# Keeping the low parts of layer 1's weights in DRAM, and casting them on ScalarE

## The chip, the cores and the metric

The kernel runs on one core of one Trainium2 chip. The metric is the device time of one execution in microseconds; three runs of the kernel before have a median of 985.02 us (984.18 to 985.11). Engines are named as in the profile: PE is the matrix engine (TensorE, PEld its weight loads), DVE is VectorE, ACT is ScalarE, POOL is GpSimd, SP is SyncE, which issues nearly all transfers.

## The reference

A decoder trunk of two layers over 1024 positions and 1024 channels, in float32. Layer 0 mixes by causal pooling, layer 1 by attention in a window of 128 with one sink per head.

```python
# layer 0
h = rmsnorm(x) * (1 + scale) + shift            # shift, scale, gate = silu(c) @ ada_w + ada_b
u, z = split(h @ w_in)                          # 2 x 2048 channels
y = group_matmul(causal_multiscale_pool(u)) * a_scale
x = x + gate * ((y * silu(z)) @ w_out)          # the output product of layer 0
# one K and V for layer 1, from x
kv = (rmsnorm(x) * kv_g * (1 + kscale) + kshift) @ w_kv
# layer 1
q, z = split(h @ b_w_in)                        # 16 heads of 64
o = windowed_attention(q, k, v, rel_bias, sinks)
x = x + gate * ((o * silu(z)) @ b_w_out)
return rmsnorm(x) * final_g
```

## The kernel before

**High and low parts.** PE multiplies in a shortened form of float32. So that the product keeps its precision, every operand is split in two: a high part (the value cast to that form) and a low part (the value less its high part). A product is three matmuls: high by high, high by low, low by high. Activations are split once. A weight tile is 128 x 1024 (512 KB); it is loaded as `raw`, ScalarE casts it to `wh`, and VectorE subtracts to `wl`. The tags `raw`, `wh` and `wl` have two buffers each.

**The stages.** Until about 424 us come the input products and the pooling of layer 0. From 424 to 565 us runs layer 0's output product: 16 steps, `order` = (n, hf), n the block of 128 output channels and hf the half of the inputs; steps with n < 5 compute both halves q of the positions (48 matmuls), the last six only the first half (24 matmuls). The second half of n = 7, 6, 5 follows until about 599 us (`last_chunk`), beside the first normalisation for layer 1. Each step needs one weight tile from `wao`. Beside the steps, `ada_step` loads a row block of the modulation weights (`ada_rest`) into a `tmp` tile, and VectorE takes its dot product with c (L239). The list ADA says how many after each step. `tmp` has three buffers, used in turn.

**Layer 1** is a list `specs` of steps that PE runs in this order. For each half q of the positions and each group r of four heads: `queries` (two weight tiles of `wb`), `gates` (two), and `start`, which sets the attention of the four blocks of 128 positions going; `attend` is a generator whose parts (scores; transposes of the probabilities; product with V) are put between the matmuls of later steps at times of a counted clock. `keys` and `values` use `wkv`. `project_out(q, part)` multiplies the attention's output by the four weight tiles `wbo[part]`; `residual` (L686) adds it to x, and for part 1 ScalarE squares the new x and GpSimd adds up the squares in `sqh` (L195). `stats` has PE sum `sqh` over the channels (L142) for the last normalisation; `finish` applies it and stores. The weights of `wbo[1]` are loaded twice: once in steps, once by `load_last` into kept tiles `wo` that the last steps (`out_quarter`) use.

**Who sets the order.** In the output product and in layer 1 the order of PE is as written; that of the other engines comes from a scheduler that knows costs and priorities. Every engine and SyncE's queue then run their own instructions strictly in that order.

Of the kernel before, what the change touches and what calls it, by code (L numbers as in the profile page):

```python
# [12 lines left out]
F32 = mybir.dt.float32  # L13
# [5 lines left out]
P = 128  # L19
D = 1024  # L20
T = 1024
# [24 lines left out]
ADA = (0, 0, 0, 2, 4, 4, 4, 4, 4, 4, 1, 1, 1, 1, 0, 0)  # L46

ENDS = (0, 1, 3, 5, 7)

# [6 lines left out]
def trunk(ctx, tc, xT, c, pack, ada_first, ada_rest, wu0_in, wg0_in, wa, wg, wao, wkv,  # L56
# [8 lines left out]
    sp = ctx.enter_context(tc.tile_pool(name="small", bufs=2))  # L65
    pp = ctx.enter_context(tc.tile_pool(name="psum", bufs=1, space=PSUM))

    BANKS = {"d": 4, "S": 2, "tp": 1, "o": 1}
# [64 lines left out]
    def load_w(src):  # L133
        return split_w(*fetch(src))

    def rstd_stats(sq, n, more=None):
# [81 lines left out]
    with ExitStack() as sa:  # L218
# [580 lines left out]
        with tc.manual_schedule(engines={ET.PE}):  # L799
# [29 lines left out]
            def half_w(n, hf):  # L829
                return load_w(wao[n, hf])  # L830

            def g_acts(hf):
# [3 lines left out]
                     + [(n, hf) for n in range(2, KT) for hf in range(2)])  # L836
            ws, outs = {}, {}
            ws[0, 0] = half_w(0, 0)
            gather(4, 5, 6, 7)
            for i, (n, hf) in enumerate(order):  # L840
# [14 lines left out]
                for _ in range(ADA[i]):  # L855
                    ada_step()
                if hf == 1:
                    for q in qs:
                        residual(n, q, outs[n][q], 16)
                    for q in qs:  # L860
                        square_add(n, q)
            assert rest_at[0] == len(rest_cols)
            mod_scale(8, 56, C_KVG)
# [150 lines left out]
    def keys(q, hk, ps=None):  # L1014
# [9 lines left out]
        if ps is not None:  # L1024
            return done(ps)
        return wkv[0], lambda w: gemm_steps(w, 0, hk, KT, done)

    vts = {}

    def values(q, hk, ps=None):  # L1030
        def done(ps):
            vts[q] = bp.tile([P, H], F32, tag="ol", name="vt", bufs=1)
            nc.scalar.copy(out=vts[q], in_=ps)
        if ps is not None:
            return done(ps)
        return wkv[1], lambda w: gemm_steps(w, 0, hk, KT, done)

# [14 lines left out]
    def queries(q, r, j, h1):  # L1052
        def run(w):
# [12 lines left out]
            yield from gemm_steps(w, 0, h1, KT, done)  # L1066
        return wb[2 * r + j], run

    def gates(q, r, j, h1):
        def run(w):  # L1070
# [10 lines left out]
            yield from gemm_steps(w, 0, h1, KT, done)  # L1081
        return wb[8 + 2 * r + j], run

# [82 lines left out]
    def out_part(q, part, n2):  # L1166

        def run(w):
            acts = lambda k, i: qts[q, 2 * part + k // 2][:, k % 2, i, :]
            for i in range(2):  # L1170
# [6 lines left out]
                yield from gemm_steps(w, i * 512, acts, 4, done)  # L1177
        return wbo[part, n2], run

# [148 lines left out]

    def woven(l, at):

        r = []
        for i, x in enumerate(l):
            r.append(x)
            if i in at:
                r.append(bare(load_last))
        return r

    keys(0, hk0, got["pswk"])
# [24 lines left out]
    with tc.manual_schedule(engines={mybir.EngineType.PE}):  # L1363
        srcs = [i for i, sp_ in enumerate(specs) if sp_[0] is not None]
        loaded = {srcs[0]: got["wq"]}
        for i, (src, run) in enumerate(specs):
# [65 lines left out]
```

## Time and profile before

| | |
|---|---|
| median of 3 runs | 985.02 us |
| profiled execution | 984.87 us |
| its span, first to last instruction | 982.6 us |
| PE, VectorE, ScalarE, GpSimd busy | 961.9, 775.7, 458.1, 145.0 us |
| granted clock of PE | 0.996 |
| read from HBM, written to it | 111.2 MB, 13.6 MB |

Busy times are those of the engine with anything running, so PE's 98% says that it is seldom idle, not that it is at its peak. A row of a window gives, for a stretch of the span, busy time and instructions of each engine, the clock, the share of time that the 16 DMA engines were busy, and what they moved. A row of waits gives who waited for whom: us in total, times, longest.

### The profile page before, as it was taken

To read this page: it belongs to the slowest core of one execution; us is meant where nothing else is said; L and a number is where in the kernel's file an instruction comes from. 1 tells how busy PE (TensorE), PEld (TensorE's weight loads), DVE (VectorE), ACT (ScalarE), POOL (GpSimd) and SP (SyncE) were. 2 spreads that over 40 slices of the span, in tenths; PEclk is the share of its full clock that TensorE was granted. 3 is DMA by queue.
4 is the path that set the end of the run, shared out by engine and by line. 5 is a ranking of instruction groups with operands and counts; after the bars stand their busy time and mean duration, and the time that the engine had idled before them with its cause. 6 is when DMAs were issued, how large, how long until landed. Compare 5 with 4: busy or idle time off the path is not lost.

```text
span 982.6 us, 12696 instructions
## 1 busy us (share of the span) xinstructions
PE 961.9 (98%) x4538; PEld 801.2 (82%) x4538; DVE 775.7 (79%) x1411; ACT 458.1 (47%) x902; POOL 145.0 (15%) x173
## 2 busy tenths in 40 slices
PE   8999999999999999999999999999999999999996
PEld 6788888888888887888888888877888888887786
DVE  5897978677978699676782278599899878889985
ACT  6534434333433244551111145486677546566544
POOL 2100000000000000000000000052324313335723
PEclk9999999999999999999999999999999999999998
DMA  9453622264225411779861223222211221223222
GB/s 331 183 174 114 192 103 65 78 201 150 65 85 194 150 64 57 262 267 327 305 216 65 86 64 130 86 65 69 82 66 64 87 86 65 64 88 106 86 87 86
DMA packets 40625, 125.67 MB, mean 128 GB/s; under 512 B 4465, under 2 KB 6641, under 8 KB 40434
## 3 DMA queue, kind: packets, MB, share of 16 engines
q1 hardware_dynamic: 40416, 123.82, 37.6%
q10 hardware_dynamic: 146, 1.05, 0.3%
q8 instruction: 35, 0.57, 0.2%
q14 instruction: 28, 0.23, 0.1%
HBM read 111.22 MB, written 13.63 MB: 127 GB/s over the span
## 4 chain that ended last, share of the span: by engine, by line
PE 78%; DVE 16%; issue 2%; ACT 2%; POOL 1%; DMA 0%; POOLq 0%; DVEq 0%; SPq 0%; ACTq 0%
PE ps_d L214 14%; PE ps_S L214 9%; PE ps_d L636 9%; PE ps_d L203 6%; PE ps_d L204 6%; PE ps_d L205 6%; PE ps_S L636 4%; PE ps_o L214 4%; PE ps_tp L214 3%; DVE wl L123 2%; PE ps_d L374 2%; PE ps_o L636 2%; PE ps_tp L636 2%; DVE tmp L542 2%; PE ps_tp L1125 1%
## 5 line engine op out<-in xcount | busy, mean ns | idle before, releaser
L121 ACT CAST wh<-raw 128x1024 fp32r<-128x1024 f32 x73 | 76.5, 1048 | 101.4 <-PE ps_d L214 78.5
L123 DVE TENSOR_TENSOR wl<-raw,wh 128x1024 fp32r<-128x1024 f32 x73 | 94.2, 1290 | 26.7 <-ACT wh L121 22.8
L203 PE MATMUL ps_d<-hm,wh 128*128 128x512 f32 x288 | 113.8, 395 | 0.0
L205 PE MATMUL ps_d<-hm,wl 128*128 128x512 f32 x288 | 112.4, 390 | 0.3 <-DVE wl L123 0.3
L204 PE MATMUL ps_d<-hm,wh 128*128 128x512 f32 x288 | 112.4, 390 | 0.0
L239 DVE CUSTOM_DVE_ANT_0 tmp<-tmp,cact,pk 128x1024 f32<-128x1024 f32 x48 | 60.7, 1282 | 33.2 <-DMA tmp<-ada_rest 32.9
L214 PE MATMUL ps_d<-gh,wh 128*128 128x512 f32 x224 | 82.0, 389 | 0.0
L214 PE MATMUL ps_S<-gh,wh 128*128 128x512 f32 x192 | 64.5, 390 | 0.0
L205 PEld LDWEIGHTS ps_d<-hm,wl 128*128 128x128 f32 x288 | 54.1, 188 | 12.6 <-DVE wl L123 1.1
L636 PE MATMUL ps_d<-hs,ws 128*128 128x512 f32 x264 | 63.4, 389 | 0.0
L1115 ACT ACTIVATE pt<-pt,nm 128x129 f32<-128x129 f32 x128 | 50.2, 394 | 26.8 <-DVE nm L1111 24.6
L203 PEld LDWEIGHTS ps_d<-hm,wh 128*128 128x128 f32 x288 | 54.1, 188 | 10.2
L204 PEld LDWEIGHTS ps_d<-hm,wh 128*128 128x128 f32 x288 | 54.2, 188 | 10.0
L636 PEld LDWEIGHTS ps_d<-hs,ws 128*128 128x128 f32 x264 | 49.5, 188 | 10.3
L542 DVE TENSOR_TENSOR tmp<-tmp 128x1039 f32<-128x1039 f32 (+3 forms) x40 | 49.4, 1235 | 6.8 <-ACT tmp L672 5.7
L612 ACT CAST ws<-tw 128x512 fp32r<-128x512 f32 x44 | 26.8, 621 | 53.9 <-PE ps_tp L214 15.1
L636 PE MATMUL ps_d<-ha,ws 128*128 128x512 f32 x216 | 51.9, 389 | 0.0
L534 POOL MEMSET tmp<- 128x16 f32 x16 | 1.7, 111 | 331.4 <-DVE tmp L542 115.9
L214 PEld LDWEIGHTS ps_d<-gh,wh 128*128 128x128 f32 x224 | 42.1, 188 | 8.7
L636 PEld LDWEIGHTS ps_d<-ha,ws 128*128 128x128 f32 x216 | 40.5, 188 | 8.4
L147 POOL TENSOR_TENSOR rs<-v,mhalf 128x4 f32<-128x4 f32 (+1 forms) x7 | 8.2, 1164 | 241.6 <-DVE v L145 241.6
L214 PE MATMUL ps_d<-gh,wl 128*128 128x512 f32 x112 | 43.6, 389 | 0.0
(294 smaller groups left out, 2492.0 us busy)
## 6 DMA issues: line engine op xcount, KB each, us to landing
tmp<-ada_rest SPq DMA_DIRECT2D x48, 512.0 KB, 4.7
raw<-wb SPq DMA_DIRECT2D x32, 512.0 KB, 3.3
raw<-wa SPq DMA_DIRECT2D x28, 512.0 KB, 3.7
raw<-wao SPq DMA_DIRECT2D x20, 512.0 KB, 4.1
ad<-ada_first SPq DMA_DIRECT2D x16, 512.0 KB, 5.0
x<-xT SPq DMA_DIRECT2D x32, 256.0 KB, 5.9
raw<-wbo SPq DMA_DIRECT2D x16, 512.0 KB, 3.3
kept_g<-tmp SPq DMA_DIRECT2D x14, 512.0 KB, 2.9
```

What stands on the lines that cost most here:

```text
L121: nc.scalar.copy(out=wh, in_=raw)
L123: nc.vector.tensor_sub(out=wl, in0=raw, in1=wh.bitcast(F32))
L203: mm(ps, lh, acts(k, 0), start=k == 0, stop=False)
L204: mm(ps, lh, acts(k, 1), start=False, stop=False)
L205: mm(ps, ll, acts(k, 0), start=False, stop=k == n - 1)
L214: mm(p, lhs, acts(k, hl, q), start=start and k == 0 and s == 0, stop=stop and k == n - 1 and s == 2)
L239: nc.vector.tensor_tensor_reduce(out=raw, in0=raw, in1=ca, scale=0.5, scalar=pk[:, bcol:bcol + 1], op0=ALU.mult, op1=ALU.add, accum_out=ad ...
L374: mm(psu[i, q], w0[k // 2][:, k % 2, w, i * P:(i + 1) * P], block(k, q)[hl], start=k == 0 and s == 0, stop=k == KT - 1 and s == 2)
L542: nc.vector.tensor_add(out=nx[:, 2 * s - 1:], in0=cur[:, 2 * s - 1:], in1=cur[:, s - 1:PAD + T - s])
L612: nc.scalar.copy(out=ws[i][:, 0, :], in_=src)
L636: mm(ps, lhs, acts(k, hl), start=start and k == 0 and s == 0, stop=k == 3 and s == 2, skip_group_check=True)
L1115: nc.scalar.activation(pt[:, i, :P + 1], pt[:, i, :P + 1], AF.Exp, bias=nm[:, i:i + 1], scale=-1.0, accum_out=den[:, i:i + 1])
```

## The change

Three things, in layer 0's output product and in layer 1:

- Behind the steps of the output product, `stage` makes the low part of 18 weight tiles of layer 1 (all 16 of `wb`, both of `wkv`): load into a `tmp` tile, cast on ScalarE into a `stage` tile, subtract on VectorE, store to a tile in DRAM (`kept_l`). The list STAGED says how many after each step.
- In layer 1 a weight whose low part is kept is loaded as two tiles, raw and low part, and ScalarE casts both. Weights are fetched two steps ahead instead of one, with a second pair of raw buffers (`raw1`). The four tiles `wbo[0]` are split as before at their first use, and their low parts stored then; at the second use they are loaded.
- `wbo[1]` is loaded and split once, into the kept tiles `wo`, in the steps of `project_out(0, 1)`; `load_last` is gone. The first step of `project_out(1, 0)` now stands ahead of `project_out(0, 1)`.

```diff
+STAGED = (0, 0, 0, 0, 0, 1, 2, 3, 3, 3, 1, 1, 1, 1, 1, 1)
...
+    kp = ctx.enter_context(tc.tile_pool(name="kept", bufs=1, space=bass.MemoryType.DRAM))
...
+    kept_l = {}
+
+    def keep(key, lo):
+        kept_l[key] = kp.tile([P, 1024], F32, name="kl")
+        nc.sync.dma_start(kept_l[key], lo.bitcast(F32))
...
+            staged = [("b", i) for i in (1, 8, 9, 2, 3, 10, 11)] + [("kv", 0), ("kv", 1)] + [
+                ("b", i) for i in (4, 5, 12, 13, 6, 7, 14, 15, 0)]
+            stage_hi = []
+
+            def stage():
+
+                name, i = key = staged.pop(0)
+                raw = tmp()[:, :1024]
+                nc.sync.dma_start(raw, {"b": wb, "kv": wkv}[name][i])
+                hi = stage_hi[len(staged) % 2].rearrange("p a c -> p (a c)")
+                nc.scalar.copy(out=hi, in_=raw)
+                lo = raw.bitcast(F32R)
+                nc.vector.tensor_sub(out=lo, in0=raw, in1=hi.bitcast(F32))
+                keep(key, lo)
...
                 for _ in range(ADA[i]):
                     ada_step()
+                if STAGED[i] and not stage_hi:
+                    stage_hi += [slot("stage") for _ in range(2)]
+                for _ in range(STAGED[i]):
+                    stage()
...
-    def load_last():
-
-        raw = wp.tile([P, 1024], F32, tag="raw", name="raw")
-        nc.sync.dma_start(raw, wbo[1, len(last_w)])
-        w = hp.tile([P, 2, T], F32R, tag="h", name="wo")
-        nc.scalar.copy(out=w[:, 0, :], in_=raw)
-        nc.gpsimd.tensor_sub(out=w[:, 1, :], in0=raw, in1=w[:, 0, :].bitcast(F32))
-        last_w.append((w[:, 0, :], w[:, 1, :]))
+    def fetch_any(key):
+
+        src = (wb if key[0] == "b" else wkv if key[0] == "kv" else wbo)[key[1:]]
+        pool, tag = ((wp, "raw"), (bp, "raw1"))[fetched[0] % 2]
+        fetched[0] += 1
+        r = [pool.tile([P, 1024], F32, tag=tag, name=tag, bufs=2) for _ in range(2)]
+        nc.sync.dma_start(r[0], src)
+        if key in kept_l:
+            nc.sync.dma_start(r[1], kept_l[key])
+        return key, r
+
+    def split_any(key, r):
+
+        if key[0] == "o" and key[1]:
+            t = hp.tile([P, 2, T], F32R, tag="h", name="wo")
+            w = t[:, 0, :], t[:, 1, :]
+            last_w.append(w)
+        else:
+            w = [wp.tile([P, 1024], F32R, tag=t, name=t) for t in ("wh", "wl")]
+        nc.scalar.copy(out=w[0], in_=r[0])
+        if key in kept_l:
+            nc.scalar.copy(out=w[1], in_=r[1])
+        else:
+            nc.vector.tensor_sub(out=w[1], in0=r[0], in1=w[0].bitcast(F32))
+            if key[0] == "o" and not key[1]:
+                keep(key, w[1])
+        return w
...
-        *woven(project_out(0, 1) + project_out(1, 0)[:2], (0, 2, 4, 6)),
+        *project_out(1, 0)[:2],
+        *project_out(0, 1),
         stats(0), project_out(1, 0)[2], finish(0, 4, FINISH[0]),
...
-                    loaded[srcs[nxt]] = load_w(specs[srcs[nxt]][0])
+                    loaded[srcs[nxt]] = split_any(*raw)
+                if nxt + 1 < len(srcs):
+                    raw = fetch_any(specs[srcs[nxt + 1]][0])
```

Lines of the kernel move down by 10 at L142 and by 29 or more in layer 1, so L142 is L152 after the change, L121 and L123 are L124 and L126, and L253 is L263.

SyncE's queue, the last transfers of the output product before the change: modulation rows, then nothing but weights (`wao` those of this product, `wkv` and `wb` of layer 1).

```order
L253 DMA tmp<-ada_rest 128x1024 x6
L130 DMA raw<-wao 128x1024
L253 DMA tmp<-ada_rest 128x1024 x5
L130 DMA raw<-wao 128x1024
L253 DMA tmp<-ada_rest 128x1024 x5
L130 DMA raw<-wao 128x1024 x10
L130 DMA raw<-wkv 128x1024 x2
```

The same place after the change, from the last but two modulation rows on. `tmp<-wb` is the load of a staged tile, `kl<-tmp` the store of its low part; the first `wao` row here is the load for the last of the 16 steps.

```order
L263 DMA tmp<-ada_rest 128x1024
L133 DMA raw<-wao 128x1024
L144 DMA kl<-tmp 128x1024
L856 DMA tmp<-wb 128x1024
L263 DMA tmp<-ada_rest 128x1024
L856 DMA tmp<-wb 128x1024
L133 DMA raw<-wao 128x1024
L144 DMA kl<-tmp 128x1024
L856 DMA tmp<-wb 128x1024
L144 DMA kl<-tmp 128x1024
L856 DMA tmp<-wb 128x1024
L133 DMA raw<-wao 128x1024
L144 DMA kl<-tmp 128x1024 x2
```

Loads and stores of the staging now stand between the weights of the output product; a load into `tmp` stands there until the buffer of the third tile before it is free.

PE's rows around the statistics of the first half, before the change: the products ahead of it belong to (1, 0) (weights in `wh`, `wl`).

```order
L203 MATMUL ps_d<-qt,wh 128x512
L204 MATMUL ps_d<-qt,wh 128x512
L205 MATMUL ps_d<-qt,wl 128x512
L142 MATMUL ps_o<-invd,sqh 128x1 x4
L203 MATMUL ps_d<-qt,wh 128x512
```

After the change the products directly ahead of it are those of (0, 1) (weights in the kept `wo`), whose squares it sums.

```order
L213 MATMUL ps_d<-qt,wo 128x512
L214 MATMUL ps_d<-qt,wo 128x512
L215 MATMUL ps_d<-qt,wo 128x512
L152 MATMUL ps_o<-invd,sqh 128x1 x4
L213 MATMUL ps_d<-qt,wh 128x512
```

The 24 matmuls of one step of (1, 0) that stood between are gone from there. On VectorE, the residual of that last product (L696) after the change stands behind an attention step, and the statistics (L155) behind it:

```order
L1184 SCALAR_TENSOR_TENSOR of<-ps_o,ol 64x256 x2
L1158 TENSOR_TENSOR cur<-ps_tp,cur 128x512
L1188 TENSOR_TENSOR of<-of,szb 128x256
L1136 COPY_PREDICATED ps_S<-tri,ps_S 128x2x128 x2
L1190 TENSOR_TENSOR qt<-of,qt 128x2x128
L1140 ISA pt,nm<-ps_S,bias,nsink 128x128
...
L696 SCALAR_TENSOR_TENSOR x<-ps_d,adac,x 128x512
L1147 RECIPROCAL den<-den 128x4
L1148 TENSOR_TENSOR pt<-pt,den 128x4x128
L155 TENSOR_SCALAR v<-ps_o 128x4
```

Where the line of dots is stand three more instructions L1140 and the reads of their results. Before the change the statistics (L145) came right behind a residual of (1, 0).

More of the change, by code (lines that the diff above doesn't have):

```diff
@@ L861, in trunk @@
                         square_add(n, q)
-            assert rest_at[0] == len(rest_cols)
+            assert rest_at[0] == len(rest_cols) and not staged
             mod_scale(8, 56, C_KVG)
@@ L1025, in keys @@
             return done(ps)
-        return wkv[0], lambda w: gemm_steps(w, 0, hk, KT, done)
+        return ("kv", 0), lambda w: gemm_steps(w, 0, hk, KT, done)
     vts = {}
@@ L1035, in values @@
             return done(ps)
-        return wkv[1], lambda w: gemm_steps(w, 0, hk, KT, done)
+        return ("kv", 1), lambda w: gemm_steps(w, 0, hk, KT, done)
     def values_split(q):
@@ L1066, in run @@
             yield from gemm_steps(w, 0, h1, KT, done)
-        return wb[2 * r + j], run
+        return ("b", 2 * r + j), run
     def gates(q, r, j, h1):
@@ L1081, in run @@
             yield from gemm_steps(w, 0, h1, KT, done)
-        return wb[8 + 2 * r + j], run
+        return ("b", 8 + 2 * r + j), run
     done_blocks = set()
@@ L1177, in run @@
                 yield from gemm_steps(w, i * 512, acts, 4, done)
-        return wbo[part, n2], run
+        return ("o", part, n2), run
     def bare(f):
@@ L1216, in trunk @@
     last_w = []
-    def load_last():
-        raw = wp.tile([P, 1024], F32, tag="raw", name="raw")
-        nc.sync.dma_start(raw, wbo[1, len(last_w)])
-        w = hp.tile([P, 2, T], F32R, tag="h", name="wo")
-        nc.scalar.copy(out=w[:, 0, :], in_=raw)
-        nc.gpsimd.tensor_sub(out=w[:, 1, :], in0=raw, in1=w[:, 0, :].bitcast(F32))
-        last_w.append((w[:, 0, :], w[:, 1, :]))
+    fetched = [0]
+    def fetch_any(key):
[22 more added lines that the diff above has]
+        return w
     def stats_quarter(c):
@@ L1327, in project_out @@
         return [ready(q, part)] + [out_part(q, part, n2) for n2 in range(4)]
[L1329 to L1336, printed above, removed]
     keys(0, hk0, got["pswk"])
@@ L1365, in trunk @@
         loaded = {srcs[0]: got["wq"]}
+        raw = fetch_any(specs[srcs[1]][0])
         for i, (src, run) in enumerate(specs):
```

## The prediction, written before the change was run

> **What bounds the kernel now.** I read the page first (busy time, then the 40 slices), after it the waits of the matrix engine, and then the stages one by one.
>
> ```profile
> span 982.6 us, 12696 instructions
> PE 961.9 (98%) x4538; PEld 801.2 (82%) x4538; DVE 775.7 (79%) x1411; ACT 458.1 (47%) x902; POOL 145.0 (15%) x173
> DVE 5897978677978699676782278599899878889985
> ACT 6534434333433244551111145486677546566544
> DMA 9453622264225411779861223222211221223222
> ```
>
> PE is busy in 98% of the span, so almost all time that this change can give back is the little that PE waits for others. The slices (24.6 us each) show two different places: in slices 17 to 21 (about 393 to 516 us: the start of layer 0's output product) the DMA engines are full while VectorE and ScalarE have room; in layer 1 (from about 600 us) it is the other way round. The change moves VectorE work from the second place to the first, and pays for it in transfers. PE's waits in layer 1 are all there is to win:
>
> ```profile
> engine line waited for: us in total, times, longest us
> PE ps_tp L1125 <- DVE pt L1119: 6.1, 5, 1.6
> PE ps_tp L154 <- DVE cur L1129: 0.4, 1, 0.4
> PE ps_d L205 <- DVE wl L123: 0.3, 1, 0.3
> PE ps_S L1105 <- DVE qt L1063: 0.3, 1, 0.3
> ```
>
> That is the whole list from 599 to 972 us: 7.1 us, every row naming VectorE. The same list over the output product (424 to 565 us) is empty: there PE waits for nobody. How full the DMA engines are there, in stretches of that stage (columns: stretch, then busy us of PE, PEld, DVE, ACT, POOL, granted clock, DMA share, GB/s):
>
> ```profile
> 439.00:467.00 28.00, 28.00 (x126) 23.17 (x125) 15.06 (x23) 3.38 (x4) 0.00 (x0) 1.00 0.92 321
> 467.00:489.00 22.00, 22.00 (x99) 18.22 (x98) 18.15 (x27) 3.66 (x5) 0.00 (x0) 1.00 0.87 300
> 489.00:511.00 22.00, 22.00 (x99) 18.22 (x98) 16.54 (x27) 3.62 (x5) 0.00 (x0) 1.00 0.83 271
> 511.00:533.00 22.00, 22.00 (x99) 18.22 (x98) 6.71 (x9) 3.61 (x5) 0.00 (x0) 1.00 0.16 54
> 533.00:565.00 32.00, 32.00 (x143) 26.50 (x142) 10.81 (x13) 6.92 (x9) 0.00 (x0) 1.00 0.26 83
> ```
>
> Until 511 us the engines are 83 to 92% taken by what is there already (30 loads for the dot products of the later modulation, the weights, x); after that the queue is nearly empty for 54 us. So the added transfers have about 54 us of free queue to go into.
>
> **Part 1: the low parts made beside the output product.** Each of 18 steps adds a load of 512 KB, a cast on ScalarE, a subtraction on VectorE and a store of 512 KB. The rows that price them:
>
> ```profile
> L121 ACT CAST wh<-raw 128x1024 fp32r<-128x1024 f32 x73 | 76.5, 1048 | 101.4 <-PE ps_d L214 78.5
> L123 DVE TENSOR_TENSOR wl<-raw,wh x15: 1212/1221/1226, 425.3 to 555.3; 128x1024 fp32r<-128x1024 f32 x15
> L239 DVE CUSTOM_DVE_ANT_0 tmp<-tmp,cact,pk x30: 1276/1284/1287, 445.9 to 511.3; 128x1024 f32<-128x1024 f32 x30
> DMA packets 6521, 21.56 MB, mean 299 GB/s; under 512 B 717, under 2 KB 717, under 8 KB 6518
> q1 hardware_dynamic: 6518, 21.52, 87.4%
> tmp<-ada_rest SPq DMA_DIRECT2D x30, 512.0 KB, 4.9
> raw<-wao SPq DMA_DIRECT2D x7, 512.0 KB, 5.0
> kept_g<-tmp SPq DMA_DIRECT2D x14, 512.0 KB, 2.9
> 554.22 1.06 ACT L121 CAST wh<-raw 128x1024 fp32r<-128x1024 f32 x1 [4.34 <-PE ps_d L214]
> ```
>
> On the engines it is cheap: 18 x 1.05 = 18.9 us of ScalarE and 18 x 1.22 = 22.0 us of VectorE, where ScalarE idles most of the time. I cost that at nothing; its cover is PE's 140 us of matmuls, and between 511 and 565 us VectorE is busy only 17.5 of 54 us. The transfers are the cost. Bytes before, from 439 to 565 us: 28 x 321 + 22 x 300 + 22 x 271 + 22 x 54 + 32 x 83 = 25.4 MB. Added: 36 x 0.524 = 18.9 MB. Together 44.3 MB, all through one queue that SyncE issues in order. The weights that PE needs stand in the same queue: behind the load for the last of the 16 steps (n = 7, second half) only 12 transfers (6.3 MB) of this stage follow, so 38.0 MB must go ahead of it. Step 15's cast of wh starts at 554.22, when step 13 frees the buffer, and step 14 has 24 matmuls of 32.00/143 = 0.224 us, 5.4 us; so PE wants its weights at about 559.9. From issue to ready it takes 5.0 to land, 1.05 to cast, 1.22 to subtract: 7.3 us. The load must therefore be issued by 552.6, and 38.0 MB from 439 on in 113.6 us is 334 GB/s. Against that stand 321 GB/s (best stretch), 299 (mean of 439 to 511 us) and 299/0.874 = 342 with no gap at all. PE is late by 38.0/rate - 113.6: 4.8 us at 321, 13.5 at 299, nothing at 342. I take 310, between the two measured stretches, since the new stores keep three tmp buffers busy longer (below): 122.6 us, **9.0 us late**, range 0 to 13.5.
>
> The buffers say the same from another side. A dot product holds one of three tmp buffers for 4.9 + 1.28 = 6.2 us; a staged tile holds it for 4.9 + 1.05 + 1.22 + its store (2.9 in a quiet queue, 4.9 as an estimate from the loads in this full one) = 10.1 to 12.1 us. 30 of the one and 18 of the other are 368 to 404 us of holding, over three buffers 123 to 135 us: 439 to 562 or 574 if none ever waits. And SyncE stands still at a load whose buffer isn't free, with the weights behind it. A rule of the Trainium skill (HBM Reference, Specifications) says that a core streaming alone measures about 425 GB/s, well above its 358 share; at 425 the 38.0 MB take 89 us and this term is zero. The trace doesn't bear it out: no stretch of this stage passes 321 at 0.92 busy.
>
> **Part 2: layer 1 with 37 subtractions fewer.** VectorE does 45 weight subtractions in the steps of layer 1 now (first row below, from 599 us on); 31 + 2 (queries, gates, keys, values) and 4 (second use of the first output weights) become ScalarE casts, so VectorE loses 37 x 1.22 = 45 us and ScalarE gains 37 casts less the 4 of the weights that are loaded once: 33 x 1.05 = 35 us. GpSimd loses its 4 subtractions. PE can gain at most the 7.1 us. Where its waits lie:
>
> ```profile
> L123 DVE TENSOR_TENSOR wl<-raw,wh x45: 1186/1226/2104, 612.3 to 937.7; 128x1024 fp32r<-128x1024 f32 x45
> L123 DVE TENSOR_TENSOR wl<-raw,wh x3: 1210/1671/2089, 647.1 to 663.8; 128x1024 fp32r<-128x1024 f32 x3
> 640.00:670.00 30.00, 26.75 (x135) 22.20 (x134) 29.08 (x58) 26.16 (x50) 18.81 (x15) 1.00 0.22 71
> PE ps_tp L1125 <- DVE pt L1119: 3.3, 2, 1.6
> PE ps_tp L1125 <- DVE pt L1119: 0.5, 1, 0.5
> 888.00:926.00 38.00, 35.72 (x184) 29.91 (x184) 34.69 (x71) 22.05 (x50) 27.14 (x21) 1.00 0.31 97
> PE ps_tp L1125 <- DVE pt L1119: 2.3, 2, 1.5
> ```
>
> (The three wait rows are of 640 to 670, 670 to 690 and 890 to 926 us.) From 640 to 670 VectorE is busy 29.08 of 30 us, but ScalarE 26.16 too: three splits lie there (second row), and three more casts make it 29.3. The wait moves rather than goes; I take half of 3.3. The 0.5, the 2.3 (GpSimd's subtractions go as well) and the 0.3 for wl I let go: **4.8 us gained**, range 7.1 gained to 3.3 lost (ScalarE's queue delays the exponentials as VectorE's did). The second load of each pair lies on a queue that the slices show 1 to 3 tenths busy, and is fetched a step earlier than now: nothing. The four stores of low parts in the first output step each hold a wl buffer for some 3 us more, beside matmuls of 5.4 us: nothing.
>
> **Part 3: the statistics right behind their last product.** The new order puts the four output steps (0,1) behind the first step of (1,0), so the statistics matmul of the first half comes straight after the product that it needs. Before, 24 matmuls stood between, and it was just in time:
>
> ```profile
> 920.06 3.32 POOL L195 TENSOR_TENSOR sqh<-sqh,sq 128x512 f32<-128x512 f32 x2 [2.62 <-ACT sq L191]
> 924.04 0.95 PE L142 MATMUL ps_o<-invd,sqh 128*128 128x1 f32 x8
> 902.08 0.40 PE L203 MATMUL ps_d<-qt,wh 128*128 128x512 f32 x1
> 906.80 0.74 DVE L686 SCALAR_TENSOR_TENSOR x<-ps_d,adac,x 128x512 f32<-128x512 f32 x1
> 907.62 0.19 ACT L1115 ACTIVATION_READ_ACCUMULATOR pt<-pt,nm 128x1 f32 x1
> 908.65 0.63 ACT L191 ACTIVATE sq<-x 128x512 f32<-128x512 f32 x1
> L195 POOL TENSOR_TENSOR sqh<-sqh,sq x7: 1284/1299/2274, 898.3 to 922.1; 128x512 f32<-128x512 f32 x7
> ```
>
> GpSimd's last sum ended at 923.38, PE asked at 924.04. In the new order PE asks 9 matmuls after an attention step's scores. A round of the same kind starts at 902.08: nine matmuls later it is 904.1. But the residual of that product stands on VectorE behind the attention step's eleven instructions and ran at 906.80 to 907.54; ScalarE was through with the exponentials at 907.81, and the square waited for a cast of wo that is gone there: 907.8 to 908.4. GpSimd's sum adds 1.28: 909.7. Wait 909.7 - 904.1 = **5.5 us**; at most 6.5 with the trace's own square (909.28 + 1.28), at least 0.74 + 0.63 + 1.28 = 2.7 with VectorE's queue empty.
>
> **Sum.** 984.87 (the profiled execution; its span is 982.6, and the median of the runs is 985.02, 0.15 above) + 9.0 - 4.8 + 5.5 = **994.6 us**.
>
> **Rivals.**
> *The transfers hide.* If the queue carries 334 GB/s or more, as by the skill's rule, PE is never late in the output product: 984.9 - 4.8 + 5.5 = 985.6, no change. For it: 342 with no gap, and in the new order most stores stand behind the next loads, so that a load seldom waits for a store's subtraction. Against: no stretch above 321.
> *VectorE's queue alone held PE (faster).* With that rate, and if the backlog on VectorE is all that delays PE in layer 1, the full 7.1 us go and the statistics wait is the bare 2.7: 980.5. For it: all wait rows name VectorE. Against: ScalarE at 26.16 of 30. It decides from 334 GB/s on.
> *ScalarE becomes layer 1's bound.* The 640 to 670 stretch keeps its 3.3 and gets as much again: 994.6 + 1.65 + 3.3 = 999.6. For it: 29.3 of 30 us. Against: that slice (the 27th) is the only one at 8 tenths; in the others of layer 1 ScalarE is at 4 to 7, and 35 us over some 370 add one.
> *The three buffers throttle the queue* to the 271 GB/s of 489 to 511: 140.2 us for 38.0 MB, 26.6 late, 984.9 + 26.6 + 0.7 = 1012. For it: the longer holding; against: nothing but that last stretch.
>
> **Chances.** My forecast 0.62, ScalarE 0.10, throttled 0.06 (slower: 0.78); hidden 0.13 (within 0.2%, some 2 us, about what a measurement of this kernel can tell from no change); VectorE alone 0.09 (faster). The time is that of the likeliest, 994.6. Leaving out the throttled case and the far part of the faster one gives 983 to 1004; my forecast's own range, transfers between 321 and 299 and the other terms as they stand, is 990 to 999.
>
> **What would show it.** DMA share above 0.8 until some 580 us; PE's waits between 530 and 580 us naming the weights' split, about 9 us; one wait of the statistics matmul (L152) for GpSimd's sum, 3 to 6 us; the pt waits down to about 2 us; VectorE's busy time about 23 us less, ScalarE's 54 more. I am wrong if the DMA share falls again before 560 us with no PE wait in the output product, or if the statistics matmul doesn't wait.

## The result: 2.4% slower, and the profile after

The changed kernel takes 1010.06 us (median of 6 runs, 1005.44 to 1012.91) against 985.38 (6 runs beside them): ratio 1.0243, 95% interval [1.0213, 1.0272]. The forecast was 994.6, slower, in a range to 1004: the direction was right, the size was not. The profiled execution took 1012.91 us, the longest of the six. Its page, the lines that answer to those shown of before:

```profile
span 1011.1 us, 12845 instructions
...
PE 975.1 (96%) x4538; PEld 809.6 (80%) x4538; DVE 751.9 (74%) x1392; ACT 507.5 (50%) x953; POOL 130.0 (13%) x169
...
DVE  5897978687977898766456678487778756778484
ACT  6534434333433344532223345687877667776344
...
PEclk9999999999999999999998999999999999999898
DMA  9453611353135314698778944633434543442022
```

The engines moved as forecast: VectorE 23.8 us less, ScalarE 49.4 more (54 forecast), and the DMA engines stay full until slice 23 (about 580 us). The row of PE's clock has two more 8s than before, where only the last slice had one:

```profile
PEclk9999999999999999999999999999999999999998
```

The largest waits of PE in the changed kernel from 424 to 1000 us (us in total, times, longest):

```profile
PE ps_o L152 <- POOL sqh L205: 4.4, 1, 4.4
PE ps_S L224 <- DVE wl L126: 3.7, 1, 3.7
PE ps_o L224 <- DVE wl L126: 3.1, 1, 3.1
PE ps_tp L1154 <- DVE pt L1148: 2.7, 3, 2.0
PE ps_d L214 <- POOL hm L177: 2.3, 1, 2.3
PE ps_d L213 <- ACT hm L169: 1.8, 1, 1.8
PE ps_o L152 <- DVE sqh L205: 1.4, 1, 1.4
PE ps_tp L224 <- DVE wl L126: 1.0, 1, 1.0
...
```

The statistics wait is there (first row), so are the output product's weights (`wl`, 7.8 us), and layer 1 has waits for the modulated activations `hm` that it did not have. The waits for `pt`, the attention's probabilities, went from 6.1 to 2.7 us. (`cur` and `prev` below are their transposes for a block of positions and the block before it.) The stretches of the output product again (PE, PEld, DVE, ACT, POOL, clock, DMA share, GB/s):

```profile
439.00:467.00 28.00, 28.00 (x125) 23.21 (x124) 16.22 (x24) 4.60 (x6) 0.00 (x0) 1.00 0.94 339
467.00:489.00 22.00, 22.00 (x98) 18.21 (x98) 13.07 (x20) 5.37 (x6) 0.00 (x0) 1.00 0.75 252
489.00:511.00 22.00, 21.00 (x93) 17.02 (x92) 12.19 (x17) 5.45 (x7) 0.00 (x0) 1.00 0.79 258
511.00:533.00 22.00, 18.92 (x78) 15.24 (x77) 13.52 (x18) 6.22 (x7) 0.00 (x0) 0.92 0.75 274
533.00:565.00 32.00, 28.35 (x114) 22.87 (x113) 21.13 (x27) 11.00 (x12) 0.00 (x0) 0.89 0.91 327
```

The clock column reads 0.92 and 0.89 where all was 1.00 before. The time that this costs stands in no row of waits, so I took all of PE's matmul starts: each start less the one before, less the median for that shape. An excess over 0.4 us I call a wait; one of 0.04 to 0.4 us, mostly matmuls that take 0.42 instead of 0.22 us, slow matmuls. In us:

| place | waits before | after | slow before | after | in all |
|---|---|---|---|---|---|
| 0 to 60 us (code unchanged) | 4.3 | 4.3 | 3.9 | 6.2 | +2.3 |
| 500 to 600 (output product) | 0.0 | 9.8 | 0.2 | 6.3 | +15.9 |
| 600 to 930 (layer 1) | 7.8 | 9.8 | 4.0 | 4.9 | +2.9 |
| from 930 (statistics, end) | 2.6 | 7.1 | 1.4 | 3.9 | +7.0 |

That is 28.1 of the 28.5 us between the two spans. The first row is not the change's: of the kernels run here, all alike up to 388 us, five had a slow stretch there in their profiled execution (this one, and below those of staging alone, of the old order, of the transfers and of the engine work).

### The profile page after: what moved, and what is told of

Its sections match the earlier page's. It is cut to its first block, busy times and chain, and to the rows that moved or that the text cites. A ratio compares the mean times of both kernels' runs of the same rounds, so it can differ in the third digit from the quotient of the medians.

```text
span 1011.1 us, 12845 instructions
## 1 busy us (share of the span) xinstructions
PE 975.1 (96%) x4538; PEld 809.6 (80%) x4538; DVE 751.9 (74%) x1392; ACT 507.5 (50%) x953; POOL 130.0 (13%) x169
## 4 chain that ended last, share of the span: by engine, by line
PE 63%; DVE 15%; DMA 11%; ACT 6%; issue 3%; POOL 2%; SPq 0%; DVEq 0%; POOLq 0%; ACTq 0%
PE ps_d L646 9%; PE ps_d L213 7%; PE ps_d L214 7%; PE ps_d L215 7%; PE ps_d L224 7%; DMA tmp<-ada_rest 5%; PE ps_S L224 4%; PE ps_S L646 4%; DMA tmp<-wb 2%; PE ps_d L384 2%; PE ps_o L646 2%; PE ps_tp L224 2%; PE ps_tp L646 2%; DVE tmp L249 2%; DMA kl<-tmp 2%
## 5 line engine op out<-in xcount | busy, mean ns | idle before, releaser
L224 PE MATMUL ps_S<-gh,wh 128*128 128x512 f32 x192 | 67.2, 405 | 0.0
L552 DVE TENSOR_TENSOR tmp<-tmp 128x1039 f32<-128x1039 f32 (+3 forms) x40 | 49.4, 1234 | 6.8 <-ACT tmp L682 5.7
L1268 ACT CAST wh<-raw 128x1024 fp32r<-128x1024 f32 x41 | 42.8, 1045 | 13.5 <-issue 7.7
L124 ACT CAST wh<-raw 128x1024 fp32r<-128x1024 f32 x28 | 29.5, 1052 | 31.3 <-PE ps_d L224 20.6
L224 PEld LDWEIGHTS ps_S<-gh,wh 128*128 128x128 f32 x192 | 37.6, 197 | 8.0
```

The lines of the kernel that those rows point to most:

```text
L124: nc.scalar.copy(out=wh, in_=raw)
L224: mm(p, lhs, acts(k, hl, q), start=start and k == 0 and s == 0, stop=stop and k == n - 1 and s == 2)
L552: nc.vector.tensor_add(out=nx[:, 2 * s - 1:], in0=cur[:, 2 * s - 1:], in1=cur[:, s - 1:PAD + T - s])
L1268: nc.scalar.copy(out=w[0], in_=r[0])
```

## The experiments

### Each part alone

Staging alone (the kernel before, with `stage()` and STAGED put into the output product and nothing else):

> The kernel before (985 us) with the 18 staged tiles added beside the output product as in the changed kernel, and layer 1 left as it was (the stored low parts are not used). Theory A (the waits of PE for late weights, 8 us, and 5 to 6 us more because the granted clock falls to 0.9 behind each wait): 985 + 14 to 16 = 999 to 1001 us, and the clock at 511 to 599 us below 0.96. Theory B (only the waits count, and the slower matmuls of 511 to 599 us came from something in layer 1's preparation): 985 + 8 to 9 = 993 to 994 us with a clock of 1.00 there.

1002.43 us, ratio 1.0171 [1.0150, 1.0192]. From 500 to 600 us: 10.9 us of waits, 4.5 of slow matmuls. Theory A, 1.4 us above its range.

Layer 1 alone:

```diff
+    for i_ in range(16):
+        kept_l["b", i_] = wb[i_]
+    for i_ in range(2):
+        kept_l["kv", i_] = wkv[i_]
...
-                if STAGED[i] and not stage_hi:
-                    stage_hi += [slot("stage") for _ in range(2)]
-                for _ in range(STAGED[i]):
-                    stage()
```

> Layer 1 as changed, but nothing is staged in the output product: the second tile of each pair is loaded from the raw weights instead of from the stored low parts, so the output has wrong low parts and the transfers, casts and order of layer 1 are those of the changed kernel. Theory A (layer 1 has by itself some 10 us of new waits: 4.5 statistics, 5 at 670 to 700 us, 3 at 738 to 777, a slower clock after them, less 7 old ones): 985 + 8 to 11 = 993 to 996 us, and no PE wait between 500 and 590 us. Theory B (layer 1's new waits at 670 to 700 us come from the lateness of the output product): 985 - 5 + 4.5 = 985 us.

995.8 us, 1.0118 [1.0092, 1.0144]. Nothing from 500 to 600 us, and the same waits for `hm` and the statistics as in the changed kernel. Theory A: layer 1's loss is its own.

The order of the output steps undone:

```diff
-        *project_out(1, 0)[:2],
         *project_out(0, 1),
+        *project_out(1, 0)[:2],
```

> The changed kernel (1010.1 us) with the four output steps (0,1) put back ahead of the first step of (1,0), so that 24 matmuls stand again between the last product and the statistics matmul. Theory (the 4.5 us that the statistics matmul waits for GpSimd's sum near 950 us are a cost of the order): the wait goes, 1010.1 - 4.5 = 1005.6 us, up to 1.5 less if the granted clock falls after that wait. Rival (the sum was late for another reason, or the work behind it waits in turn): above 1008.5.

1002.11 us, 1.0178 [1.0148, 1.0208]. The statistics wait is gone. From 930 us on the waits fall from 7.1 to 2.6 and slow matmuls from 3.9 to 1.5: 6.9 us, where 4.5 is the wait itself. The median is 2 us below the theory's lowest figure (1004.1), which took 1.5 for the slow matmuls.

Layer 1 alone, with the old order as well:

> Layer 1 as changed but with the old order of the output steps, and nothing staged (raw weights stand in for the low parts, as in the run of layer 1 alone, 1.0118 of before). Theory A (the statistics wait and the slow matmuls behind it, 4.5 + 2.5 us, are all that the order costs; the rest of layer 1 loses 4 us by itself): 995.8 - 7 = 988 to 990 us, above before. Theory B (with the order undone layer 1 gains, as forecast, 4.8 us): 980 to 983 us.

990.76 us, 1.0061 [1.0046, 1.0077]. Theory B, which is the forecast's part 2, falls: without staging and without the new order, the rest of the change in layer 1 still costs about 6 us, with the same waits for `hm`. Staging 17, that rest 6 and the order 6 (from the pairs above) make 29, where the change costs 24; with intervals of 2 to 3 us each, that is as near as they add.

### The output product: engine work, transfers, buffers, queues

Only the engine work of the staging, from a resident tile (against `stage` of staging alone):

```diff
-                raw = tmp()[:, :1024]
-                nc.sync.dma_start(raw, {"b": wb, "kv": wkv}[name][i])
...
-                nc.scalar.copy(out=hi, in_=raw)
-                lo = raw.bitcast(F32R)
-                nc.vector.tensor_sub(out=lo, in0=raw, in1=hi.bitcast(F32))
-                keep(key, lo)
+                nc.scalar.copy(out=hi, in_=cact)
+                nc.vector.tensor_sub(out=hi, in0=cact, in1=hi.bitcast(F32))
```

> The kernel before with only the engine work of the staging: 18 casts on ScalarE and 18 subtractions on VectorE, from a tile that is resident, no load and no store. Theory (18.9 and 22.0 us of engine work lie wholly beside PE's matmuls): within 1 us of before, no PE wait between 500 and 590 us. Rival (the longer queues of the two engines alone make the weights late): 988 us or more.

985.7 us, 0.9999 [0.9990, 1.0008]. The 41 us of engine work (18.9 and 22.0) are free.

Only its transfers (`keep(key, raw)` directly behind the load):

> The kernel before with only the transfers of the staging beside the output product: 18 loads into tmp tiles and 18 stores of them (raw, not low parts; not used later), no cast and no subtraction. With both, the time was 1.0171 of before (+17 us). Theory A (the staged casts and subtractions, waiting in ScalarE's and VectorE's queues for their loads, hold up the splits of the output product's weights behind them): without them PE waits under 2 us between 500 and 590 us, 985 to 989 us. Theory B (the dot products alone, late because of the transfers, hold up the weights' subtractions, or the weights' loads themselves are late): waits of 6 to 9 us with 4 us of slow matmuls, 996 to 1003 us.

998.97 us, 1.0127 [1.0105, 1.0149]. Theory B. Here the forecast's mechanism stands alone. PE's longest wait in this kernel, 424 to 960 us:

```profile
PE ps_d L223 <- ACT wh L124: 8.2, 1, 8.2
```

The cast that it waits for, in ScalarE's order of time (start, length, and in brackets the idle time before it and who ended it):

```profile
554.75 1.04 ACT L124 CAST wh<-raw 128x1024 fp32r<-128x1024 f32 x1 [12.85 <-DMA raw<-wao]
```

and the stretches ahead of it:

```profile
467.00:489.00 22.00, 22.00 (x98) 18.21 (x97) 11.09 (x16) 3.38 (x4) 0.00 (x0) 1.00 0.90 315
489.00:511.00 22.00, 22.00 (x98) 18.21 (x97) 10.76 (x15) 3.38 (x4) 0.00 (x0) 1.00 0.87 306
511.00:533.00 22.00, 22.00 (x99) 18.21 (x98) 9.01 (x15) 3.37 (x4) 0.00 (x0) 1.00 0.88 309
```

ScalarE sits idle for 12.85 us until the weights land, and PE waits 8.2 us for their cast; the queue moves 306 to 315 GB/s, and 310 was the rate assumed.

In the changed kernel the weights wait in another place. Its order of time, ScalarE first:

```profile
514.12 1.06 ACT L124 CAST wh<-raw 128x1024 fp32r<-128x1024 f32 x1
```

and VectorE, the four instructions that matter:

```profile
517.68 1.28 DVE L249 CUSTOM_DVE_ANT_0 tmp<-tmp,cact,pk 128x1024 f32<-128x1024 f32 x1 [2.44 <-DMA tmp<-ada_rest]
...
521.15 1.28 DVE L249 CUSTOM_DVE_ANT_0 tmp<-tmp,cact,pk 128x1024 f32<-128x1024 f32 x1 [2.18 <-DMA tmp<-ada_rest]
...
525.61 1.29 DVE L249 CUSTOM_DVE_ANT_0 tmp<-tmp,cact,pk 128x1024 f32<-128x1024 f32 x1 [3.16 <-DMA tmp<-ada_rest]
...
528.14 1.21 DVE L126 TENSOR_TENSOR wl<-raw,wh 128x1024 fp32r<-128x1024 f32 x1
```

The weights had landed and were cast by 515.18. Their subtraction ran 13 us later, because three dot products stood ahead of it on VectorE, each waiting for a load (and two residual sums behind the last of them). PE wanted it from 526.2 on. This is read from the trace; an order of VectorE with the weights' subtraction ahead of the dot products was not run. Instead I put the weights' subtractions on GpSimd, idle there:

```diff
...
-                return load_w(wao[n, hf])
+                return split_w(*fetch(wao[n, hf]), nc.gpsimd)
```

> The changed kernel (1010.1 us), except that the low parts of the output product's own weights (16 steps) are subtracted on GpSimd, which is idle there, at 2.65 us each instead of 1.22. Transfers and their order are the same. Theory A (in the trace the weights of the late steps have landed and been cast 9 to 14 us before PE needs them; their subtraction stands on VectorE behind dot products that wait for their own loads): PE's waits of 8.2 us between 500 and 590 us fall below 1.5, and with them 4 to 5 us of slowed matmuls: 996 to 999 us. Theory B (the forecast's: the weights' loads come late through the queue): the waits stay at 6 to 9 us and now name GpSimd, 1007 to 1011 us.

1028.5 us, 1.0435 [1.0415, 1.0455]: worse, so both theories' numbers miss. PE's largest waits from 500 to 600 us now name ScalarE's cast:

```profile
PE ps_S L224 <- ACT wh L124: 11.2, 2, 8.7
```

and ScalarE's order of time shows why:

```profile
544.02 1.04 ACT L858 CAST stage<-tmp 128x1024 fp32r<-128x1024 f32 x1 [12.80 <-DMA tmp<-wb]
545.72 1.04 ACT L858 CAST stage<-tmp 128x1024 fp32r<-128x1024 f32 x1 [0.66 <-DMA tmp<-wb]
546.67 1.04 ACT L124 CAST wh<-raw 128x1024 fp32r<-128x1024 f32 x1
```

The weights' cast stands behind staged casts that wait 12.8 us for theirs. In both versions something that waits for the same full queue stands ahead of the weights' split. But this run does not decide how much of the changed kernel's waits the dot products ahead on VectorE make: it moved the wait to ScalarE, and took some 2.4 to 2.7 us for most of the subtractions instead of 1.22.

The buffers, which I had made a rival: the low part is written over the high part and stored from the `stage` tile, so `tmp` is free sooner.

```diff
-                lo = raw.bitcast(F32R)
-                nc.vector.tensor_sub(out=lo, in0=raw, in1=hi.bitcast(F32))
-                keep(key, lo)
+                nc.vector.tensor_sub(out=hi, in0=raw, in1=hi.bitcast(F32))
+                keep(key, hi)
```

> The changed kernel (1010.1 us), except that the low part is written over the high part in the stage tile and stored from there: the same bytes in the same queue, but a tmp buffer is free after the subtraction and not only after the store (some 4 us less for each of 18 tiles, 72 of about 390 us of holding). Theory A (the three buffers throttle the queue: loads stand behind stores, 0.75 of the DMA engines' time from 467 to 533 us): the share rises above 0.85, PE's waits for wl fall from 8.2 to under 3 us and the time to 997 to 1002 us. Theory B (the DMA engines' rate is the limit, whatever the buffers): 1009 to 1011 us with the same waits.

1010.78 us, 1.0262 [1.0235, 1.0289]: no gain. Yet the queue ran better. Packets of 439 to 560 us, in the changed kernel:

```profile
DMA packets 10594, 35.45 MB, mean 293 GB/s; under 512 B 1175, under 2 KB 1175, under 8 KB 10588
```

and here:

```profile
DMA packets 10950, 37.81 MB, mean 312 GB/s; under 512 B 1215, under 2 KB 1215, under 8 KB 10943
```

The buffers do throttle, by 6% (five other runs with all 18 tiles staged through `tmp` have 291 to 295 GB/s), but PE's waits from 500 to 600 us stay at 8.9 us (9.8 in the changed kernel). The `stage` tiles are now held until their store, and staged casts on ScalarE wait for that, 4.95 and 2.77 us, besides 8.49 us for a load. So the run shows that the buffers slow the queue, not what a faster queue alone would give.

### The clock

The statistics wait, filled with 18 useless matmuls (4.0 us):

```diff
+            if q == 0:
+                ps = bank("d")
+                for k in range(18):
+                    mm(ps, last_w[3][0][:, :P], qts[0, 2][:, 0, 0, :], start=k == 0, stop=k == 17)
```

> The changed kernel (1010.1 us) with 18 matmuls more (4.0 us of useless work on PE) directly ahead of the statistics matmul, in the place where PE waits 4.5 us. Theory A (a wait of more than some 2.5 us makes the clock drop, and the next 8 to 17 matmuls take 0.42 instead of 0.22 us): the wait is under 0.7 us, the matmuls behind it run at 0.22 us at once, and the time is 2 to 2.5 us less, 1007.7 us. Theory B (the slow matmuls belong to that place, not to the wait): they stay, 1010 us.

1002.24 us, 1.0179 [1.0156, 1.0202]: more work, less time, and less than either theory gave. In the profiled execution, from 930 us on, waits and slow matmuls fall from 11.0 to 4.2 us for 4.0 of added work, a gain of 2.8 us as in theory A; the rest of the difference lies in the output product, where this execution had 5.9 us less. The instructions of every engine and of SyncE's queue stand there in the same order in both traces, so that part does not come from an order that the edit changed; with this same order five profiled executions lose between 10.2 and 16.1 us in the output product. Why the median gained 7.8 us, 5 more than the filled wait explains, stays open. Then three waits of set length in the kernel before:

```diff
+                if i in (9, 11, 13):
...
+                    nc.scalar.copy(out=held[0][:, 0, :], in_=outs[n][0])
+                    for _ in range((i - 7) // 2):
+                        nc.scalar.copy(out=flat, in_=cact)
+                    mm(next_bank(), held[0][:, 0, :P], held[0][:, 1, :], start=True, stop=True)
```

> The kernel before with three waits put into PE's order in the output product, where it had none: behind steps 9, 11 and 13 one more matmul needs a chain of 2, 3 and 4 copies on ScalarE that starts when the step's products end, so PE waits about 1.7, 2.7 and 3.8 us. Theory A (the clock drops behind a wait longer than some 2.5 us): no slow matmul behind the first, 5 to 13 matmuls at 0.42 instead of 0.22 us behind the second and third, 984.5 + 8.2 + 3 to 5 = 996 to 998 us. Theory B (the slow matmuls of the changed kernel come from full DMA queues or late weights, not from the wait): all matmuls behind the three waits at 0.22 us, 993 us.

999.13 us, 1.0142 [1.0123, 1.0160]. The waits were 2.4, 3.7 and 2.5 us, and not one slow matmul came behind them: theory A in that form is wrong. A wait of 2.4 us for the statistics at 580 us, which the delay brought about, did have six slow matmuls behind it (its stretch counts 2.29 us as busy, but eight of the matmuls in it have one column; how such matmuls count was not tried). What tells them apart shows in stretches of 3.41 us, whose borders I set where the clock changes; all changes of one execution lie on one such grid. First the changed kernel, at the wait of 3.24 us that ends at 529.40 and at the statistics:

```profile
525.47:528.88 3.41, 0.86 (x4) 0.38 (x2) 3.27 (x5) 1.26 (x3) 0.00 (x0) 1.00 0.31 105
528.88:532.29 3.41, 2.89 (x7) 2.31 (x8) 3.41 (x6) 1.98 (x3) 0.00 (x0) 0.50 0.93 364
532.29:535.71 3.42, 3.42 (x17) 2.81 (x16) 1.82 (x3) 0.55 (x1) 0.00 (x0) 1.00 0.84 310
...
945.31:948.72 3.41, 0.81 (x4) 0.35 (x2) 3.08 (x14) 2.26 (x10) 1.96 (x2) 1.00 0.00 0
948.72:952.13 3.41, 1.62 (x8) 1.62 (x8) 0.61 (x1) 0.20 (x1) 1.45 (x1) 0.50 0.00 0
952.13:955.55 3.42, 3.42 (x10) 2.74 (x10) 0.16 (x1) 0.00 (x0) 1.02 (x1) 0.50 0.00 0
955.55:958.96 3.41, 3.41 (x17) 2.79 (x16) 0.75 (x1) 0.00 (x0) 0.00 (x0) 1.00 0.00 0
```

and the kernel with three waits, at the one of 3.71 us that ends at 550.11:

```profile
544.92:548.33 3.41, 1.64 (x8) 1.02 (x6) 0.89 (x1) 1.93 (x3) 0.00 (x0) 1.00 0.30 117
548.33:551.75 3.42, 1.65 (x7) 1.39 (x8) 1.69 (x3) 2.22 (x3) 0.00 (x0) 1.00 0.49 158
551.75:555.16 3.41, 3.41 (x17) 2.83 (x16) 0.00 (x0) 0.00 (x0) 0.00 (x0) 1.00 0.00 0
```

Where PE was busy for 0.81 or 0.86 of 3.41 us, the next stretch runs at half clock (0.50), and a second one follows the one with 1.62 us, but not the one with 2.89. The wait of 3.71 us fell across a border and left 1.64 and 1.65 us of work on either side: no drop. So what counts is how empty one stretch of the grid is; length and place of the wait decide together.

The 17 profiled executions of this document say the same. I counted the stretches at full clock from 60 us on that hold no one-column matmul. All 25 in which PE was busy 1.43 us or less are followed by half clock. Of 19 with 1.49 to 1.78 us six are, one of them with 1.64 us (old order, 666.73 us). From 1.81 us on none is. At half clock, a stretch with 2.58 us or less was followed by another at half clock every time, one with 2.89 us or more never. With four or eight one-column matmuls in a stretch at full clock, half clock came behind up to 2.61 us. The border between is not sharp in busy time, and why is open. The grid lies at another place of the program in each execution, so the same wait can cost slow matmuls in one execution and none in the next.

The Trainium skill (TensorE: Matmul & The Clock Gate, Part 1, What's actually happening) states such a free-running window of 3413 ns. The trace agrees with its length; but here a window that was a quarter busy was enough.

### Layer 1: why the casts cost

One of ScalarE's two passes over the second half's first modulation given back to VectorE (`m.act` false for `hk1`):

> The changed kernel (1010.1 us), except that one of ScalarE's two passes over each of the 8 tiles of the second half's first modulation (0.81 us each, 662 to 695 us) goes back to VectorE. Theory A (these tiles are late because ScalarE has the casts of the weights in its queue): PE's waits of 2.0 + 2.6 us at 692 to 696 us fall below 1.5 in total and the slowed matmuls behind them go too: 1004 to 1006 us. Theory B (VectorE, busy 18.7 of 20 us there, or GpSimd's part of the chain is the limit): the waits stay within 1 us or become waits for pt, 1009 to 1012 us.

1010.34 us, 1.0246 [1.0208, 1.0285]. Theory B: the waits for `hm` go, and the row `PE ps_tp L1154 <- DVE pt L1148` grows from 2.7 to 6.6 us. The same tiles due sooner (`PREP` 2.0 for 2.6):

> The changed kernel (1010.1 us) with the 8 tiles of the second half's first modulation due 2.0 us apart instead of 2.6 (the last one 4.2 us sooner). Theory A (those tiles stand too late in ScalarE's and GpSimd's queues behind the casts of weights): PE's waits of 4.6 us at 692 to 696 us and 1.8 us of slow matmuls behind them go: 1003 to 1005 us. Theory B (moving them up moves other work down): as much is waited for attention tiles instead, 1008 to 1012 us.

1007.36 us, 1.0222 [1.0195, 1.0250]: between the theories. The `hm` waits give way to smaller ones (4.0 us for `pt`, 2.5 for `prev` and `cur`), and the drop of the clock there goes; against the changed kernel the intervals overlap.

Six tiles staged where the queue had been empty, with the old order:

```diff
-STAGED = (0, 0, 0, 0, 0, 1, 2, 3, 3, 3, 1, 1, 1, 1, 1, 1)
+STAGED = (0, 0, 0, 0, 0, 0, 0, 0, 0, 0, 1, 1, 1, 1, 1, 1)
...
+            staged = [("b", i) for i in (2, 3, 10, 11)] + [("kv", 0), ("kv", 1)]
```

> Staging for 6 tiles only (queries and gates of the second group of heads, keys and values), one behind each of the steps 10 to 15, where the queue stood at 0.16 to 0.26 before; the old order of the output steps; the rest as changed. Theory A (staging is free where the queue is empty, and the casts of layer 1 take away some of the 4.8 us of waits at 656 to 706 us that the kernel without staging still has): 979 to 982 us, no PE wait over 1 us between 500 and 590 us. Theory B (with the second tile's cast on ScalarE the second half's first modulation is late again, 4.6 us of waits and 1.8 us of slow matmuls): 984 to 988 us.

986.24 us, 1.0007 [0.9995, 1.0019]. Half of each theory: staging is free there (no wait from 500 to 600 us), and the `hm` waits come with only six weights cast on ScalarE. PE's largest waits from 424 to 960 us:

```profile
PE ps_d L214 <- POOL hm L177: 2.3, 1, 2.3
PE ps_d L213 <- ACT hm L169: 1.9, 1, 1.9
```

and ScalarE in order of time (the exponentials between left out):

```profile
671.90 1.04 ACT L1267 CAST wh<-raw 128x1024 fp32r<-128x1024 f32 x1
672.85 1.04 ACT L1269 CAST wl<-raw 128x1024 fp32r<-128x1024 f32 x1
...
674.75 0.80 ACT L169 ACTIVATE hm<-xn,adac,acol 128x512 fp32r<-128x512 f32 x1
...
676.23 0.80 ACT L173 ACTIVATE xn<-xn,adac,acol 128x512 f32<-128x512 f32 x1
```

The last tile's two passes stand behind both casts of a weight and run between an attention block's exponentials. With the same transfers, but the second cast on VectorE (`nc.vector.tensor_copy`):

> The kernel with six staged tiles and the old order (986.2 us), except that the copy of a kept low part runs on VectorE again instead of ScalarE; loads, stores and staging are the same. Theory A (the second cast in ScalarE's queue makes the second half's first modulation late: 2.0 + 2.6 us of waits and 1.6 us of slow matmuls at 675 to 679 us): those waits fall below 1 us, the waits of the transposes for VectorE (1.8 + 1.8 + 0.7 us) come back, 982 to 984 us. Theory B (the second load of each pair, or the order of the fetches, makes them late): the waits at 675 to 679 us stay, 985.5 to 988 us.

983.23 us, 0.9977 [0.9968, 0.9986], and PE's largest waits from 424 to 970 us:

```profile
PE ps_o L1176 <- POOL cur L1165: 2.0, 1, 2.0
PE ps_tp L1153 <- DVE pt L1147: 0.9, 3, 0.5
```

The time is theory A's: the transfers are innocent, the second cast in ScalarE's queue is what makes `hm` late. This was tried with six tiles; the changed kernel with all 18 has the same two rows for `hm`, but its second casts were not moved back to VectorE. The waits for `pt` did not come back as expected; one for `cur` took their place.

### A version that beats both

The changed kernel without staging and with the old order:

> The changed kernel without staging (the weights of queries, gates, keys and values are split on VectorE as before) and with the old order of the output steps: left are the fetch two steps ahead, the first output weights' low parts kept at their first use, and the second output weights loaded and split once. Theory A (what the change gains in layer 1 without its costs is the waits near 900 to 920 us, 2.6 us): 982 to 983.5 us against 984.5. Theory B (casts on ScalarE instead of subtractions on VectorE move the waits to another place): 985 to 988 us.

982.62 us against 986.08, 0.9965 [0.9955, 0.9975]: 0.35% faster than before. The waits for `pt` at 900 and 920 us are gone, as in theory A, and no drop of the clock shows ahead of the last 8 us, which run at half clock in the kernel before too. What is left of the change here is the loading and splitting once of the last output weights, the kept low parts of the first, and the fetch two steps ahead.

## Why the prediction was wrong, step by step

Two steps failed: the 4.8 us gained in layer 1, which came out as a loss, and the matmuls behind each wait, which the sum has at nothing.

- **"38.0 MB ... I take 310 ... 9.0 us late"** (part 1): the size of the waits was right, 9.8 us in the profiled execution, 1.6 of it for the statistics matmul behind; in five other executions with all 18 tiles staged and the weights split as in the change 7.9 to 10.9. The transfers alone gave the mechanism and the rate (306 to 315 GB/s). In the changed kernel it acts through VectorE's order: weights that are there wait behind dot products that are not (read from its trace; no run isolates it). That the size fits is partly luck: its queue moved a mean of 293 GB/s from 439 to 560 us, and by the forecast's formula that makes 129.7 - 113.6 = 16 us, where 8.2 were waited for weights. The 18.9 and 22.0 us of engine work cost nothing, as forecast.
- **The rival of the three buffers** had a real rate (252 to 274 GB/s from 467 to 533 us), but not the time: its 26.6 us of lateness were 8.2. Raising the rate to a mean of 312 gave no time back, in a run that held the `stage` tiles longer instead. Its 1012 us is near the result by luck. That the transfers hide is refuted: the best of these stretches in any run was 351 GB/s at 0.97 busy, and PE waited whenever the transfers of 18 tiles were there. The 425 GB/s of the Trainium skill (HBM Reference, Specifications) was not seen.
- **"4.8 us gained"** (part 2): this step failed. From 600 to 930 us PE's waits rose from 7.8 to 9.8, and the change to layer 1 without the other two costs about 6 us. The waits for `pt` did shrink, by 3.4 us of the 4.8. The forecast knew that ScalarE would be full from 640 to 670 us and took half of one wait off for that. But the new waits are not for the exponentials that it priced: they are for the next normalised tiles, `hm`, whose two passes on ScalarE and one on GpSimd have PE waiting at the end of the chain. That rival, "ScalarE becomes layer 1's bound", was nearest, at the wrong place.
- **"5.5 us"** (part 3): the wait was 4.5, as forecast in kind and within 2.7 to 6.5; with its slow matmuls the order cost 6.9 in the profiles.
- **What is in no term of the sum**: the matmuls behind a wait. This is the largest part of the miss, and the forecast put it at nothing without a word: it priced each wait at its length. From 500 us on slow matmuls cost 9.5 us more than before (6.1, 0.9 and 2.5), and that the waits cause them is shown by the filled wait and by the stretches of the grid. In before, the clock fell only for the last 8 us, behind the last statistics; no row quoted in the forecast showed a price for it.

By the same table, 984.9 + 9.8 + 2.0 + 4.5 of waits, + 9.5 of slow matmuls, + 2.3 at the start is 1013.0, the profiled 1012.9; this takes that one execution apart and is no second test. Of the 18.3 us between the forecast and it, 9.5 are slow matmuls, 6.8 are part 2 (2.0 lost for 4.8 gained) and 2.3 the start; parts 1 and 3 were off by 0.8 and 1.0, in opposite directions.

Open: why staging with engine work (17 us) costs more than its transfers alone (12.5) when their profiled executions are 2 us apart; the intervals nearly touch.

## What to carry to other kernels

Room on an engine does not hide work that needs transfers: here 41 us of engine work alone cost nothing, its transfers alone 13 us, both together 17. Look at what will stand behind the loads, in the queue and on each engine, and put the transfers where the queue is empty (six tiles there made no wait, 18 beside full traffic cost 17 us). When work moves from one engine to another, follow the tiles that the second engine was making on time, not its busy share. Price a wait of the matrix engine at its length plus the slow matmuls that can come behind it (here 1.5 us behind a wait of 3.24).

## What the hardware showed unexpectedly

PE's clock is set on a fixed grid of 3.41 us: each stretch from 60 us on in which it was busy 1.43 us or less led to half clock for at least the next one; of those at full clock and without one-column matmuls, 1.49 to 1.78 us did in six cases of 19 and more never. A wait of 3.24 us cost 1.5 us more through this, one of 3.71 us nothing. And 4.0 us of useless matmuls in a wait took 2.8 us off the last stage of the profiled execution.
